# Few-token and heavy expert parts by turns, with a third gate and up buffer and down parts loaded by GpSimd

## The chip, the cores and the metric

The kernel runs on one core of one Trainium2 chip. The metric is the device time of one execution in microseconds, as the median of several runs. The engines are TensorE (PE in the rows), VectorE (DVE), ScalarE (ACT), GpSimd (POOL) and SyncE (SP, which here only issues transfers); PEld is the loading of TensorE's weights.

## What is computed

A two-layer diffusion block on 256 latent and 256 context tokens of width 1024. Each layer has a mixer (attention, pooling, retention) and a channel mixer. The first layer's channel mixer is dense; the second is a mixture of eight experts, of which each token takes two. The change is in the experts alone:

```
def swiglu(t, wg, wu, wd):
    return (jax.nn.silu(t @ wg) * (t @ wu)) @ wd

def moe_ffn(t, router, wg, wu, wd):
    ...
    logits = (tf @ router).astype(jnp.float32)
    top_v, top_i = lax.top_k(logits, TOP_K)
    top_w = jax.nn.softmax(top_v, axis=-1)
    gates = jnp.sum(jax.nn.one_hot(top_i, N_EXPERTS, dtype=jnp.float32) * top_w[..., None], axis=1)
    y = jnp.zeros_like(tf)
    for e in range(N_EXPERTS):
        y = y + gates[:, e:e + 1] * swiglu(tf, wg[e], wu[e], wd[e])
    return y.reshape(shape)
```

All is in float32; `wg` and `wu` are 1024 x 2816, `wd` is 2816 x 1024 for each expert.

## The kernel before

The weights of an expert come in 11 units (`FC`), 88 in all (`NU`). A unit is 256 of the 2816 hidden columns: a gate and up part of 128 x 4096 (2,048 KB, buffers `RGU`, `rgu` in the rows) and a down part of 128 x 2048 (1,024 KB, buffers `RAW`, `raw`). Two buffers of each stand in turn, unit u in buffer u % 2; `load_gu` and `load_d` (lines 1513 to 1521) issue the loads on SyncE's queue, two units ahead, as soon as a buffer is free.

The kernel counts each expert's tokens, sorts the experts by it, and branches (`arms`, line 2528) to a plan that fits the counts. A **heavy** expert has up to 128 tokens in a place. Its weights are split on chip into a high and a low half (`split`: ScalarE copies the high half, VectorE subtracts it for the low half; `ghi`, `glo` for gate and up, three pairs of buffers of 128 x 2048; `dhi`, `dlo` for down, two pairs), and each product is three passes of TensorE (`mm3`): 24 products of 128 x 512 for gate and up and 12 for down in each unit. A **few-token** expert (class `Few`, up to 64 tokens) takes its weights as they are, as the moving operand, with no split.

For each unit there are these steps: `inner` (gate and up products, eight blocks of 128 columns of the input), `act` (silu on ScalarE, times up on VectorE, tile `hx`), `turn` (TensorE flips `hx`; for a heavy unit, `flips`, ScalarE and VectorE then split the flipped tile into `SP`; for a few-token unit VectorE copies it), and `outer` (down products, summed in a PSUM bank over the expert's units). The unit `behind` is the one whose `act`, `turn` and `outer` are still to come; they stand within the next unit's slot.

With the input's counts the plan is: expert 0 alone, in the shadow of other work; `group` (lines 2270 and on), in which expert 1, in two halves, is heavy and experts 2 and 3 are few-token, unit by unit; then `places` (line 2140), which takes experts 4 (few-token), 5 and 6 (heavy) and 7 (few-token) one after the other, 44 units. In `places`, a few-token unit's own `act`, `turn` and `outer` stand in its own slot. A heavy unit's `split_g` and `split_d` stand in its own slot too: the second half of gate and up and the down part are split while TensorE works on the first half, and the down part is used a slot later. Small steps that gather the next expert's tokens or add the last one's result to the residual (generators in `side`, taken by `aside`) are scattered between. Near the end sixteen GpSimd operations (`XT` in the rows) work on the residual.

The order of instructions on each engine is the order in which the program emits them; semaphores and the reuse of buffers make them wait.

Of the kernel before, what the change touches and what calls it, by code (L numbers as in the profile page):

```python
# [36 lines left out]
E = 8  # L37
# [300 lines left out]
def build(tc, a, dbg=None):  # L338
# [1157 lines left out]
    RD = RAW  # L1496
# [21 lines left out]
    def load_d(u):  # L1518
        if u < NU:
            for c in ((slice(0, 1024), slice(1024, 2048)) if u == NU - 1 else (slice(0, 2048),)):  # L1520
                Y.dma_start(RD[u % 2][:, c], src_of(u)[:, 4096:][:, c])
# [11 lines left out]
    def first_d(u):  # L1533
        p = PLACES[u]
        return P5 if u == 5 else AHEAD[p - 2][2] if p > 1 else RD[p]
# [12 lines left out]
    def split_g(u, i, parts=1):  # L1548
        if u < NU:
            q = (2 * part.get(u, u) + i) % 3  # L1550
            n = 2048 // parts
            for j in range(parts):
                c = slice(n * j, n * j + n)
                split(RGU[u % 2][:, 2048 * i:2048 * i + 2048][:, c], GHI[q][:, c], GLO[q][:, c])
                yield ("rest",)
            if i == 1 and not stream:
                load_gu(u + 2)

    def split_d(u, parts=1, eng=None):
        if u < NU:  # L1560
            n = 2048 // parts
            for j in range(parts):
                c = slice(n * j, n * j + n)
                split(RD[u % 2][:, c], DHI[u % 2][:, c], DLO[u % 2][:, c], eng)
                yield ("rest",)
            load_d(u + 2)
# [206 lines left out]
    def gate_up(u, x, ks, b=None):  # L1773
        if b is None:
            b = BK[4 + 2 * (u % 2)]
        for k in ks:
            q = (2 * part.get(u, u) + k // 4) % 3
# [22 lines left out]
    def down_to(acc, w, ht, c):  # L1800
        for kk in range(2):
            for hf in range(2):
                sl = slice(1024 * kk + 512 * hf, 1024 * kk + 512 * hf + 512)
                mm3(acc[hf], ht[:, 0, 128 * kk:128 * kk + 128], ht[:, 1, 128 * kk:128 * kk + 128],
                    DHI[w][:, sl], DLO[w][:, sl], c == 0 and kk == 0, c == FC - 1 and kk == 1)

    def down_e(u, ht):
        s, c = divmod(u, FC)
        down_to(accs(s), u % 2, ht, c)
# [77 lines left out]
    def finish(few, acc, x, rows, last):  # L1887
# [18 lines left out]
        room = RGU[NU % 2]  # L1906
# [234 lines left out]
    def places(todo, side, begun=False):  # L2141
# [10 lines left out]
        def inner(u, ks):  # L2152
            if kinds[u // FC]:
                few_of(u).gate_up((RGU[u % 2][:, :2048], RGU[u % 2][:, 2048:]), ks, bank_of(u))
# [15 lines left out]
        def outer(u):  # L2170
            s, c = divmod(u, FC)
            if kinds[s]:
                few_of(u).down(RD[u % 2], c)
                load_d(u + 2)
            else:
                down_to(accs(s), u % 2, before.pop(), c)
# [10 lines left out]

        behind = None
        for s, few in todo:
            for c in range(FC):  # L2190
# [6 lines left out]
                if not few:  # L2197
                    run(split_g(u, 0, 2))
# [5 lines left out]
                if not few:  # L2204
                    run(split_g(u, 1, 2))
                    rows = split_d(u, 2)
                    next(rows)
                if behind:
                    turn(behind)
                if not few:  # L2210
                    aside(2 if c < 9 else 8)
                inner(u, range(4, 8))
                if not few:
                    run(rows)
                if behind:
                    outer(behind)
                behind = u
                if few:
                    load_gu(u + 2)
                    if u < NU - 1:  # L2220
# [6 lines left out]
                        behind = None  # L2227
                if c == 0 and s > todo[0][0]:
# [21 lines left out]

    def one_hot_few(pos, m):
# [18 lines left out]
    def group(s, few, m, then):  # L2270
# [5 lines left out]
        units = []  # L2276
        for c in range(FC):
            units.append((0, c))
            units += [(1 + i // FC, i % FC) for i in range(len(few) * c, len(few) * c + len(few))]
        stream.update({u0 + i: (([s] + few)[j], c) for i, (j, c) in enumerate(units)})  # L2280
        end = u0 + len(units)
        part.update({u0 + n * c: u0 + c for c in range(FC)})
        nxt = s + 1 + len(few)
        x = nxt % 2
# [19 lines left out]
        def few_in(u, ks):  # L2304
            f.gate_up((RGU[u % 2][:, :2048], RGU[u % 2][:, 2048:]), ks, BK[4])
            if ks[-1] == KT - 1:
                load_gu(u + 2)
                f.swish(BK[4])

        def few_out(u):  # L2310
            f.down(RD[u % 2], units[u - u0][1])
            load_d(u + 2)
# [27 lines left out]
        if s > 1:  # L2340
# [3 lines left out]
            load_gu(u0 + 2)  # L2344
            gate_up(u0, 1, range(4, 8), BK[6])
            run(split_d(u0))
        else:
            one_hot_few(pos_of(few[0]), m)
            from_stash(m)
        swish(BK[6], HX[2])  # L2350
# [24 lines left out]
        for c in range(FC):  # L2375
# [26 lines left out]
            down_to(HEAVY[0][2], u % 2, hts[0], c)  # L2402
# [5 lines left out]
            down_to(HEAVY[1][2], u % 2, hts[1], c)  # L2408
# [10 lines left out]
            if c < FC - 1:  # L2419
                load_gu(u + n + 2)  # L2420
                run(split_d(u + n))
        stream.clear()
        part.clear()
# [112 lines left out]
    def expert_of(s):  # L2536
        eid[s] = nc.values_load(CNTI[0:1, 1, s:s + 1], engines=[ET.SP], min_val=0, max_val=E - 1)

    def parts_of(s):
        for i in range(2):  # L2540
            lookup[FC * s + 1 + i] = nc.values_load(CNTI[0:1, 2 + i, s:s + 1], engines=[ET.SP], min_val=0, max_val=NU - 1)
# [4 lines left out]
    def first_twice():  # L2546
# [10 lines left out]
    load_gu(FC)  # L2557
    load_d(FC)
    parts_of(1)
    load_gu(FC + 1)  # L2560
    load_d(FC + 1)
    arm = arm_of(C1[0:1, 0:1], 7)

    def next_first():
# [3 lines left out]
        for s in (3, 5):  # L2568
            parts_of(s)
# [3 lines left out]
        run(split_d(FC))  # L2573

    few_ends = [(s, s in (4, 7)) for s in (4, 5, 6, 7)]
# [36 lines left out]
```

## Time and profile before

| | |
|---|---|
| median of 3 runs | 1586.68 us (1580.56 to 1586.84) |
| profiled execution | 1585.11 us |
| its span | 1583.3 us |
| TensorE busy | 1460.4 us (92%) |
| VectorE, ScalarE, GpSimd busy | 812.8, 612.7, 93.8 us |
| the group (expert 1 with 2 and 3) | 905 to 1177 us |
| expert 4 (few-token) | 1179.8 to 1269.1 us |
| experts 5 and 6 (heavy) | 1269.1 to 1478.9 us |
| expert 7 (few-token) | 1478.9 to 1563.5 us |
| end of the output | 1583.3 us |

The profiled execution is 1.6 us under the median. Stages are told from the tile names: a product `bk<-rgu,hx` with 64 columns of weights is a few-token unit of experts 4 and 7, `bk<-ghi` a heavy unit. Nearly all rows have the same line, 281, a helper's, so they are read by tile. A few-token product stands as two records in the trace.

### The profile page before, as it was taken

How to read it: one execution, taken by the hardware profiler on the slowest of the kernel's cores; microseconds unless marked ns; L12 is line 12 of the kernel's file. 1: busy time of each engine (PE TensorE's matmuls, PEld its weight loads, DVE VectorE, ACT ScalarE, POOL GpSimd, SP SyncE). 2: the span in 40 equal slices, each digit the busy share in tenths (PEclk: the TensorE clock that was granted, in tenths of full speed). 3: DMA queues.
4: the chain of work that ended last, by engine and by line, in shares of the span. 5: the costliest groups of instructions: out<-in, count | busy, mean ns of one | idle time of the engine just before them, and what ended most of it. 6: DMA issues, size and time to landing. Idle time of an engine off the chain costs nothing. (4 is left out here: it accounts for less than half of the span.)

```text
span 1583.3 us, 25008 instructions
## 1 busy us (share of the span) xinstructions
PE 1460.4 (92%) x10228; PEld 1085.1 (69%) x10228; DVE 812.8 (51%) x1468; ACT 612.7 (39%) x1122; POOL 93.8 (6%) x105
## 2 busy tenths in 40 slices
PE   6989998999999999887988799999998889999986
PEld 4646687887787888674766577777765468877643
DVE  4564446666554353766445542434232087988402
ACT  3465444522223443355542132323320066776201
POOL 2310002000000510100000100000000000000110
PEclk9999999999999999999999899999999999999998
DMA  9535333455765132331479799999989998988894
GB/s 381 181 136 211 107 107 107 133 202 182 255 239 184 56 133 94 115 129 38 161 300 421 283 374 387 352 376 375 359 338 364 389 357 316 364 328 322 326 404 176
DMA packets 45698, 398.35 MB, mean 252 GB/s; under 512 B 5600, under 2 KB 5856, under 8 KB 8960
## 3 DMA queue, kind: packets, MB, share of 16 engines
q1 hardware_dynamic: 44640, 391.98, 65.1%
q0 software_dynamic: 640, 4.26, 0.7%
q8 instruction: 84, 1.38, 0.3%
q10 hardware_dynamic: 288, 0.36, 0.1%
q14 instruction: 46, 0.38, 0.1%
HBM read 395.53 MB, written 1.05 MB: 250 GB/s over the span
## 5 line engine op out<-in xcount | busy, mean ns | idle before, releaser
L281 PE MATMUL b<-HH,wh 128*128 128x512 f32 (+1 forms) x752 | 267.2, 355 | 9.0 <-ACT wh L281 7.5
L281 PE MATMUL b<-HH,wl 128*128 128x512 f32 (+1 forms) x752 | 259.7, 345 | 1.6 <-DVE wl L281 1.5
L281 PE MATMUL b<-HL,wh 128*128 128x512 f32 (+1 forms) x752 | 259.0, 344 | 1.1 <-DVE HL L281 1.1
L281 DVE TENSOR_TENSOR wl<-raw,wh 128x512 fp32r<-128x512 f32 x228 | 151.3, 702 | 130.7 <-ACT wh L281 130.4
L281 ACT ACTIVATE wh<-raw 128x512 fp32r<-128x512 f32 x228 | 131.8, 622 | 183.5 <-DMA raw<-in_fgu_dram 122.0
L281 PE MATMUL bk<-ghi,HL 128*128 128x512 f32 x528 | 181.6, 407 | 8.1 <-ACT ghi L281 8.1
L281 PEld LDWEIGHTS b<-HH,wh 128*128 128x128 f32 x752 | 144.5, 192 | 49.7 <-issue 21.4
L281 DVE TENSOR_TENSOR glo<-rgu,ghi 128x1024 fp32r<-128x1024 f32 x132 | 154.7, 1218 | 16.4 <-ACT ghi L281 16.2
L281 PEld LDWEIGHTS b<-HH,wl 128*128 128x128 f32 x752 | 144.4, 192 | 21.7 <-DVE wl L281 4.6
L281 PEld LDWEIGHTS b<-HL,wh 128*128 128x128 f32 x752 | 144.8, 192 | 17.5 <-DVE HL L281 1.9
L281 DVE TENSOR_TENSOR hx<-hx,bk 128x256 f32<-128x256 f32 (+2 forms) x88 | 29.5, 336 | 235.1 <-ACT hx L281 235.1
L281 ACT ACTIVATE hx<-bk 128x256 f32<-128x256 f32 (+3 forms) x89 | 28.4, 319 | 307.2 <-PE bk L281 307.1
L281 ACT ACTIVATE ghi<-rgu 128x1024 fp32r<-128x1024 f32 x132 | 131.2, 1051 | 18.9 <-DMA rgu<-in_moe_dram 18.8
L281 PEld LDWEIGHTS bk<-ghi,HL 128*128 128x128 f32 x528 | 101.4, 192 | 37.0 <-ACT ghi L281 9.2
L281 PE MATMUL bk<-dhi,SP 128*128 128x512 f32 x352 | 120.1, 402 | 0.0
L281 PE MATMUL b<-h,wh 128*128 128x512 f32 (+1 forms) x384 | 111.9, 375 | 0.0
L281 PE MATMUL bk<-glo,HL 128*128 128x512 f32 x264 | 105.3, 399 | 1.5 <-DVE glo L281 1.3
L281 DVE TENSOR_TENSOR dlo<-raw,dhi 128x1024 fp32r<-128x1024 f32 (+1 forms) x55 | 78.8, 1434 | 15.8 <-ACT dhi L281 15.8
L281 PE MATMUL bk<-rgu,hx 128*32 128x128 f32 (+1 forms) x1376 | 77.2, 305 | 6.5 <-DVE hx L281 3.5
L281 PEld LDWEIGHTS b<-h,wh 128*128 128x128 f32 x384 | 69.8, 188 | 16.4 <-issue 2.5
L281 PEld LDWEIGHTS bk<-rgu,hx 128*32 128x32 f32 (+1 forms) x1376 | 52.9, 118 | 37.8 <-issue 14.1
L281 PEld LDWEIGHTS bk<-dhi,SP 128*128 128x128 f32 x352 | 66.1, 188 | 17.4 <-issue 1.6
(339 smaller groups left out, 2178.3 us busy)
## 6 DMA issues: line engine op xcount, KB each, us to landing
rgu<-in_moe_dram SPq DMA_DIRECT2D x81, 2048.0 KB, 9.5
raw<-in_moe_dram SPq DMA_DIRECT2D x80, 1024.0 KB, 7.2
raw<-in_wmod_dram SPq DMA_DIRECT2D x40, 1024.0 KB, 4.9
raw<-in_fgu_dram SPq DMA_DIRECT2D x22, 1024.0 KB, 5.0
p<-in_moe_dram SPq DMA_DIRECT2D x16, 1024.0 KB, 14.0
raw<-in_wout_dram SPq DMA_DIRECT2D x12, 1024.0 KB, 4.9
raw<-in_fd_dram SPq DMA_DIRECT2D x11, 1024.0 KB, 4.9
raw<-in_wib_dram SPq DMA_DIRECT2D x9, 1024.0 KB, 5.1
```

The costliest lines, as they stand in the source:

```text
L281: r = f(*args, **kw)
```

## The change

The last four experts of this plan (44 units) are taken by turns. `order_by_turns` sets the order of the units: in the first 37 slots, H for heavy and F for few-token, it is `HHFHFHHFHFHHFHFHHFHFHHFHFHHFHFHHFHFHF` (22 H, 15 F; a heavy follows a few-token unit 14 times and a heavy one 7 times), then seven few-token units of expert 7. `by_turns` replaces `places` on this plan. The other parts:

- A third gate and up buffer, two tiles in the room of the second `dhi` and `dlo` pair; it is filled by two loads of 1,024 KB. There is one `dhi`, `dlo` pair now. Buffers are handed on: `done_gu` and `done_d` load the next unit not yet asked for into the buffer that has come free.
- The down parts' loads are issued on GpSimd's queue (`G.dma_start`), so that queue also reads the experts' numbers.
- The down part of a heavy unit is split after that unit's `turn`, in the next slot, instead of in the unit's own slot. `outer` stands between the blocks 4 and 5 and the blocks 6 and 7 of the next unit. Gate and up are split ahead (`take_apart`): half a unit in the few-token slot before, or, before a few-token slot, the unit after it.
- The tokens of experts 4 and 7 are gathered in `tokens_few` directly ahead of their first unit.
- In `group` the down split and the buffers' hand-over follow the new functions, with one `dhi`, `dlo` pair.

```
-    def load_gu(u):
+    at_g, at_d = {}, {}
+    def load_gu(u, i):
+        at_g[u] = i
         if u < NU:
-            for c in ((slice(0, 2048), slice(2048, 4096)) if u == NU - 1 else (slice(0, 4096),)):
-                Y.dma_start(RGU[u % 2][:, c], src_of(u)[:, c])
+            for l, h in ((0, 2048), (2048, 4096)) if i == 2 or u == NU - 1 else ((0, 4096),):
+                Y.dma_start(RGU[i][:, l:h] if i < 2 else GU[i][l // 2048], src_of(u)[:, l:h])
...
+                G.dma_start(RAW[i][:, l:h], src_of(u)[:, 4096 + l:4096 + h])
...
+    def done_gu(u):
+        load_gu(max(at_g) + 1, at_g[u])
...
+    def by_turns(side):
...
+        take_apart(u0, 2)
+        for u in range(u0, NU):
+            s, c = stream[u]
+            last = u == NU - 1
+            if light(u) and c == 0:
+                tokens_few(s)
+            if behind:
+                act(behind)
+            inner(u, range(0, 4))
+            if behind:
+                turn(behind)
+                if not light(behind):
+                    run(split_d(behind, 2))
...
+            aside(4 if u == u0 else 3 if s == 7 and c > 3 else 2)
+            take_apart(u + 1, 2 if light(u) else 1)
+            inner(u, range(4, 6))
+            if behind:
+                outer(behind)
+            inner(u, range(6, 8))
+            if light(u):
+                done_gu(u)
+            take_apart(u + 1, 2)
+            if u + 1 < NU and light(u + 1):
+                take_apart(u + 2, 1)
+            behind = u
+            if s == 7 and c == 5:
+                aside(100)
+                for f in range(KT):
+                    G.tensor_scalar(YT[:, f], YT[:, f], MOD[1][:, 40 + f, 0:1], None, op0=OP.mult)
+                    G.tensor_tensor(XT[:, f, :T], XT[:, f, :T], YT[:, f], OP.add)
...
+    GU = [[t[:, :2048], t[:, 2048:]] for t in RGU] + [[con.tile([128, 2048], F32, name=f"gu{t}", tag=t) for t in ("wh0", "wl0")]]
...
-    DHI, DLO = ([con.tile([128, 2048], F32R, name=f"{n}{i}", tag=f"w{n[1]}{i}") for i in range(2)] for n in ("dhi", "dlo"))
+    DHI, DLO = (con.tile([128, 2048], F32R, name=n, tag=t) for n, t in (("dhi", "wh1"), ("dlo", "wl1")))
```

How the queues change, at three places. ScalarE in the heavy experts, before: one unit's worth, `ghi` a half of gate and up, `hx` the silu of the unit behind, `SP` its flipped tile, `dhi` this unit's down part.

```order
L281 ACTIVATE ghi_8925<-rgu_6257 128x1024 [waits DMAHW5_49,Activation_49]
L281 ACTIVATE ghi_8925<-rgu_6257 128x1024 [waits Activation_49]
L281 ACTIVATE hx<-bk_6474 128x256 [waits PE_49]
L281 ACTIVATE ghi_8926<-rgu_6257 128x1024 [waits Activation_49] x2
L281 ACTIVATE dhi_8930<-raw_78 128x1024 [waits DMAHW6_49,PE_49]
L281 ACTIVATE SP<-bk_6474 128x256 [waits DVE_49,PE_49]
```

After, one heavy slot and the few-token slot behind it (`hx 128x128` is the silu of the few-token unit ahead, at the heavy slot's start; `hx 128x256` is the heavy unit's own, at the few-token slot's start; `ghi` the two halves of the next heavy unit):

```order
L281 ACTIVATE hx<-bk_6474 128x128 [waits PE_49]
L281 ACTIVATE ghi_8928<-rgu_4982 128x1024 [waits DMAHW2_49]
L281 ACTIVATE ghi_8928<-rgu_4982 128x1024
L281 ACTIVATE hx<-bk_6472 128x256 [waits DVE_49,PE_49]
L281 ACTIVATE SP<-bk_6472 128x256 [waits DVE_49,PE_49]
L281 ACTIVATE dhi<-raw_78 128x1024 [waits DMASW1_49,Activation_49]
L281 ACTIVATE dhi<-raw_78 128x1024 [waits Activation_49]
L281 ACTIVATE ghi_8926<-rgu_4982 128x1024 x2
```

The down part's high half has moved from ahead of the flipped tile `SP` of the unit behind to directly after the flipped tile of its own unit, and the first half of the next unit's gate and up, which waits for its transfer, now stands ahead of the silu of the unit before it.

TensorE in the heavy experts, before, from a flip (`CA,hx`) to the down products (`dhi,SP`):

```order
L281 MATMUL bk_6472<-CA,hx 128x128 [waits DVE_49]
L281 MATMUL bk_6472<-CA,hx 128x128
L281 MATMUL bk_6474<-ghi_8926,HL 128x512 [waits Activation_49]
L281 MATMUL bk_6474<-glo_8929,HL 128x512 [waits DVE_49]
L281 MATMUL bk_6474<-ghi_8926,HL 128x512 x2
L281 MATMUL bk_6474<-glo_8929,HL 128x512
L281 MATMUL bk_6474<-ghi_8926,HL 128x512
L281 MATMUL bk_6474<-ghi_8926,HL 128x512 [waits Activation_49]
L281 MATMUL bk_6474<-glo_8929,HL 128x512 [waits DVE_49]
...
L281 MATMUL bk_6470<-dhi_8930,SP 128x512 [waits Activation_49]
L281 MATMUL bk_6470<-dlo_8932,SP 128x512
```

After, in a few-token slot behind a heavy unit (`rgu` with `hx` or `sil` are few-token gate and up products):

```order
L281 MATMUL bk_6472<-rgu_4982,hx 64x256 [waits DMAHW2_49]
L281 MATMUL bk_6472<-rgu_4982,hx 64x256 x7
L281 MATMUL bk_6474<-CA,hx 128x128 [waits DVE_49]
L281 MATMUL bk_6474<-CA,hx 128x128
L281 MATMUL bk_6472<-rgu_4982,sil 64x256 x4
L281 MATMUL bk_6468<-dhi,SP 128x512 [waits Activation_49]
L281 MATMUL bk_6468<-dlo,SP 128x512 [waits DVE_49]
```

Between the flip and the down products twelve heavy products stood before; now four few-token ones do, and the low half `dlo` is waited for.

The transfers, before: gate and up and down parts by turns on SyncE's queue.

```order
L281 DMA raw_78<-in_moe_dram 128x2048 [waits DMAHW2_49,PE_49]
L281 ISA
L281 DMA rgu_4982<-in_moe_dram 128x4096 [waits DMAHW3_49,DVE_49]
L281 ISA
L281 DMA raw_79<-in_moe_dram 128x2048 [waits DMAHW4_49,DVE_49]
```

After, GpSimd's queue near the end, with the down parts of the last units around the residual's sixteen operations:

```order
L281 DMA raw_78<-in_moe_dram 128x2048 [waits DMASW3_49,PE_49]
L281 ISA
L281 DMA raw_79<-in_moe_dram 128x2048 [waits DMASW4_49,PE_49]
L281 TENSOR_SCALAR XT<-XT,MOD_75 128x256 [waits DVE_49,Pool_49]
L281 TENSOR_TENSOR XT<-XT 128x256 [waits Pool_49]
```

The down loads have left SyncE's queue for GpSimd's, where the residual's operations now stand between them.

## Rows read from the trace of the kernel before

**Rows 1.** Stages, core 0: us from:to, length, busy times by engine, clock, DMA share.
```profile
core 0: us, PE busy (x) PEld busy (x) DVE busy (x) ACT busy (x) POOL busy (x), PEclk, DMA share, GB/s
1179.80:1269.10 89.30, 76.54 (x539) 42.45 (x539) 17.72 (x51) 8.58 (x21) 0.00 (x0) 0.98 0.94 365
1269.10:1478.90 209.80, 202.78 (x928) 164.07 (x928) 177.47 (x198) 146.01 (x185) 0.00 (x0) 0.98 0.89 339
1478.90:1563.50 84.60, 74.73 (x538) 41.81 (x538) 10.24 (x30) 7.07 (x18) 13.04 (x16) 0.98 0.89 348
1179.80:1563.50 383.70, 354.05 (x2002) 248.33 (x2003) 205.44 (x279) 161.66 (x223) 13.04 (x16) 0.98 0.90 347
905.00:1177.00 272.00, 271.25 (x2733) 202.87 (x2732) 99.15 (x154) 81.74 (x126) 0.00 (x0) 1.00 0.94 369
```

**Rows 2.** Waits 1179.8 to 1563.5: who waits for whom, us, times, longest.
```profile
PE bk L281 <- DVE hx L281: 16.7, 25, 2.9
...
DVE dlo L281 <- ACT dhi L281: 14.6, 13, 2.5
```

**Rows 3.** The SyncE queue's waits, the same stretch.
```profile
SPq L281 <- PE bk L281: 143.7, 42, 6.6
```

**Rows 4.** SyncE's issues in experts 5 and 6: start, us, what.
```profile
1347.03 0.33 SPq L281 DMA_DIRECT2D raw<-in_moe_dram  x1
...
1355.59 0.33 SPq L281 DMA_DIRECT2D raw<-in_moe_dram  x1
```

**Rows 5.** Timeline of a heavy unit: start, us, operation, idle before it.
```profile
1352.56 0.38 PE L281 MATMUL bk<-CA,hx 128*128 128x128 f32 x2
...
1352.97 0.38 ACT L281 ACTIVATE SP<-bk 128x256 fp32r<-128x256 f32 x1 [2.22 <-PE bk L281]
...
1353.25 1.05 ACT L281 ACTIVATE dhi<-raw 128x1024 fp32r<-128x1024 f32 x1
...
1353.39 0.42 DVE L281 TENSOR_TENSOR SP<-bk,SP 128x256 fp32r<-128x256 f32 x1 [0.38 <-ACT SP L281]
...
1354.33 1.23 DVE L281 TENSOR_TENSOR dlo<-raw,dhi 128x1024 fp32r<-128x1024 f32 x1 [0.52 <-ACT dhi L281]
...
1355.55 0.40 PE L281 MATMUL bk<-dhi,SP 128*128 128x512 f32 x1
```

**Rows 6.** Timeline of TensorE, a few-token unit of expert 7.
```profile
1510.73 0.33 PE L281 MATMUL bk<-CA,hx 128*128 128x128 f32 x1 [0.70 <-DVE hx L281]
1511.44 1.94 PE L281 MATMUL bk<-raw,hx 128*64 128x512 f32 x8 [0.39 <-DVE hx L281]
1513.21 1.90 PE L281 MATMUL bk<-rgu,hx 128*64 128x256 f32 x16
1514.94 1.90 PE L281 MATMUL bk<-rgu,sil 128*64 128x256 f32 x16
1517.53 0.33 PE L281 MATMUL bk<-CA,hx 128*128 128x128 f32 x1 [0.70 <-DVE hx L281]
```

**Rows 7.** Stretches: under GpSimd-issued loads; the best 25 us of the last experts.
```profile
768.00:770.00 2.00, 2.00 (x19) 2.00 (x18) 1.91 (x5) 0.97 (x2) 0.00 (x0) 1.00 1.01 430
...
1250.00:1275.00 25.00, 19.25 (x106) 10.13 (x107) 7.39 (x12) 6.35 (x8) 0.00 (x0) 0.93 1.01 426
```

**Rows 8.** Timeline of TensorE: a gather's products.
```profile
1313.16 1.98 PE L281 MATMUL bk<-og,HH 128*128 128x128 f32 x16
```

**Rows 9.** Loads issued near 876.7 and 1153.1 us: KB, us to landing.
```profile
rgu<-in_moe_dram SPq DMA_DIRECT2D x1, 2048.0 KB, 8.6
...
rgu<-in_moe_dram SPq DMA_DIRECT2D x1, 2048.0 KB, 10.5
```

**Rows 10.** Timeline at the start of expert 5.
```profile
1269.12 4.63 DVE L281 TENSOR_TENSOR glo<-rgu,ghi 128x1024 fp32r<-128x1024 f32 x4 [3.40 <-ACT ghi L281]
...
1269.14 0.51 PE L281 MATMUL bk<-ghi,HL 128*128 128x512 f32 x1 [1.43 <-ACT ghi L281]
```

**Rows 11.** The window of eight products at half clock, 1219.21.
```profile
1219.21:1222.41 3.20, 3.20 (x8) 1.00 (x10) 0.33 (x2) 0.00 (x0) 0.00 (x0) 0.50 0.87 330
```

More of the change, by code (lines that the diff above doesn't have):

```diff
@@ L1549, in split_g @@
         if u < NU:
-            q = (2 * part.get(u, u) + i) % 3
+            q = (2 * heavy(u) + i) % 3
             n = 2048 // parts
@@ L1553, in split_g, with split_d @@
                 c = slice(n * j, n * j + n)
[L1554 removed]
+                split(gu_of(u)[i][:, c], GHI[q][:, c], GLO[q][:, c])
                 yield ("rest",)
[L1556 to L1559 removed]
+            if i == 1 and u > FC:
+                done_gu(u)
+    def split_d(u, parts=1):
         if u < NU:
@@ L1776, in gate_up @@
         for k in ks:
-            q = (2 * part.get(u, u) + k // 4) % 3
+            q = (2 * heavy(u) + k // 4) % 3
             c = slice(512 * (k % 4), 512 * (k % 4) + 512)
@@ L2186, in aside, with take_apart @@
                     side.pop(0)
+        apart = {}
+        def take_apart(u, n):
+            if u < NU and not kinds[u // FC]:
+                while apart.setdefault(u, 0) < n:
+                    run(split_g(u, apart[u], 2))
+                    apart[u] += 1
         behind = None
@@ L2196, in places @@
                     continue
-                if not few:
-                    run(split_g(u, 0, 2))
+                take_apart(u, 2)
                 if behind:
@@ L2249, in places, with order_by_turns @@
         finish(few, accs(E - 1), (E - 1) % 2, rows, last)
+    def order_by_turns():
+        u0 = 4 * FC
+        many_ = [(s, c) for s in (5, 6) for c in range(FC)]
+        few_ = [(s, c) for s in (4, 7) for c in range(FC)]
+        turns = NU - u0 - 7
+        units = []
+        for i in range(turns):
+            units.append((many_ if -(-2 * FC * (i + 1) // turns) > -(-2 * FC * i // turns) else few_).pop(0))
+        units += many_ + few_
+        stream.update({u0 + i: sc for i, sc in enumerate(units)})
+        heavies = [u for u in range(u0, NU) if stream[u][0] in (5, 6)]
+        part.update({u: 2 * FC + i for i, u in enumerate(heavies)})
@@ L2268, in gather_few, with together, group @@
             yield
-    def group(s, few, m, then):
+    def together(s, few):
+        u0, n = FC * s, 1 + len(few)
+        units = []
+        for c in range(FC):
+            units.append((s, c))
+            units += [(few[i // FC], i % FC) for i in range(len(few) * c, len(few) * c + len(few))]
+        stream.update({u0 + i: v for i, v in enumerate(units)})
+        part.update({u0 + n * c: u0 + c for c in range(FC)})
+    def group(s, few, m, then, nxt=None, x=None):
         u0 = FC * s
@@ L2275, in group @@
         n = 1 + len(few)
[L2276 to L2284, printed above, removed]
+        if nxt is None:
+            nxt = s + 1 + len(few)
+            x = nxt % 2
         side = []
@@ L2572, in next_first, with rest, go @@
             gate_up(FC, 1, range(4 * i, 4 * i + 4), BK[6])
-        run(split_d(FC))
-    few_ends = [(s, s in (4, 7)) for s in (4, 5, 6, 7)]
+    buffers = []
+    def rest(*groups, body):
+        def go():
+            if not buffers:
+                buffers.extend((dict(at_g), dict(at_d)))
+            for d, o in zip((at_g, at_d), buffers):
+                d.clear()
+                d.update(o)
+            stream.clear()
+            part.clear()
+            for g in groups:
+                together(*g) if g else order_by_turns()
+            done_gu(FC)
+            body()
+        return go
     def two_groups():
```

186 lines of the change are left out of this document (137 added, 49 removed).

## Prediction

> **What bounds the kernel now.** I read the busy times by stage first. Of the last four experts' 383.70 us TensorE is busy 354.05, so it stands idle 29.65 [rows 1]: 12.76 us in expert 4 (89.30 less 76.54), 9.87 in expert 7 (84.60 less 74.73) and 7.02 in experts 5 and 6 (209.80 less 202.78). The few-token experts move 365 and 348 GB/s with TensorE waiting; the heavy pair moves 339 GB/s with TensorE full. The three-expert group ahead is TensorE's altogether (271.25 of 272.00). The waits say the same: TensorE's largest wait is for VectorE's part of the silu and of the flip (16.7 us), and VectorE's low half of a down part waits for ScalarE's high half, 14.6 us [rows 2], which costs nothing so long as TensorE is elsewhere. The SyncE queue is always early: it stands waiting for a buffer to come free, 143.7 us for TensorE alone [rows 3]. So there is at most some 30 us to be had, by laying transfer-bound parts beside TensorE-bound ones.
>
> Unit prices. A steady heavy unit takes 8.56 us from one down-part issue to the next (1347.03 to 1355.59) [rows 4]; less some 0.2 for the flip, that is 0.232 for each of its 36 products of 128x512. A few-token unit is 1.73 us for the first half of gate and up, the same for the second, 1.77 for down, and 6.81 us from 1510.73 to 1517.53 with its own waits [rows 6].
>
> **Transfers.** 37 slots and a tail of seven few-token units read 44 units of 3.15 MB (2,048 and 1,024 KB), 138 MB in all. Loads issued by GpSimd alone ran at 430 GB/s; the best 25 us here made 426 on SyncE's queue alone [rows 7]. At 426 that is 325 us: transfers would not bind as a whole. Who issues the down parts changes little, since SyncE's issues are 0.33 us each [rows 4]. What changes is that a down load no longer stands behind a gate and up load that waits for its buffer.
>
> **The turn of a heavy unit, the largest new cost.** Before, the down part is split while TensorE computes the second half of the same or next unit: from the flip at 1352.56 the high half's copy starts at 1353.25, the low half follows at 1354.33, and TensorE takes up the down product at 1355.55, about 3.05 us after the flip, with 12 products between, so that the chain is hidden [rows 5]. After, the split of a unit's down part stands on ScalarE and VectorE behind that unit's flip, one slot later, and the down product stands after only two of the four remaining blocks. Between flip and down product TensorE has 0.86 us of work in a few-token slot (1.73 / 2) or 1.38 in a heavy one (6 x 0.23), plus asides. The chain cannot start earlier, as ScalarE takes the flip's copy first. So, on TensorE:
> - few-token slot behind a heavy, 15 times: 1.73 + 3.05 + 2.57 (eleven of the twelve down products) + 0.86 = 8.2, of which 1.8 idle less what asides fill;
> - heavy behind a few-token one, 14 times: 24 x 0.23 + 0.2 + 1.77 = 7.5, no idle;
> - heavy behind heavy, 7 times: 2.78 + 3.05 + 2.57 + 1.38 = 9.8;
> - the first heavy 5.6.
>
> The 37 make 123 + 105 + 69 + 5.6 = 302.6 us.
>
> **Asides and gathers.** About 90 of the asides' 128x128 products fall in slots without a gap, at 1.98 / 16 = 0.124 us each: 11.2. The two gathers of few-token experts are now 32 products each ahead of the first few-token unit, 4.0 us, and the two one-hot writes ahead and copies behind leave TensorE about 1.7 more (two steps the size of the flip's copies, 0.38 and 0.42, on either side) [rows 5, 8]: 11.4 for both. Between 0 and 1.7 for the copies stays open.
>
> **Late gate and up parts.** Where a heavy slot stands between two few-token slots, the next heavy unit's first split goes onto ScalarE and VectorE ahead of the present unit's silu. Its buffer was given back only when the split before the last ended, in the middle of the few-token slot, so its load has about one slot of 7.5 us. A 2,048 KB load landed in 8.6 us at best here and 10.5 under load [rows 9]. VectorE's part of the silu then comes behind one high half (1.05) and two low halves (1.23 each) of the next unit and takes about 0.42 itself [rows 5]: with the gaps between them some 4.05 us after the landing. With 8.6 us I make that 3.5 us for the four whole loads (14) and 1 us for the two halved ones (2): 16. Bounds: nothing, if loads land in 7.5; 4 x 1.9 more at 10.5.
>
> **Start and tail.** The first heavy unit's split waits for the group's last VectorE work, where few-token expert 4 now starts without a split: between 1.43 us (TensorE's wait where expert 5 starts) and 4.63 (its first four low halves) [rows 10]; I take 3. The tail's seven few-token units run at 6.81 to 7.7 (84.60 / 11), say 7.0: 49. The third buffer helps only the first of them. The 16 GpSimd operations on the residual (13.04 us busy [rows 1]) now stand ahead of the down loads of the last four units in GpSimd's queue; each of those is wanted a unit or more later, so I take 0, and 4 us at most. Otherwise a down load on GpSimd waits for the last product out of its buffer, and behind it stands only the next down load. The end (last product to the last store) is unchanged. In the group, one down buffer instead of two costs 0 to 2 us, TensorE having 0.75 us free in 272.
>
> **Clock.** In one few-token unit eight down products fill 3.20 us where 1.77 is usual, at a granted clock of 0.50, the lower level of 1.2 GHz [rows 6, 11]; TensorE had waited for the flip just before. I see four spells like it in the stretch, at 1.6 us lost in each some 7 in all, about what a mean granted clock of 0.98 over 383.70 us says (7.7) [rows 1]. I leave them as they are; the change could remove them or add more where TensorE waits for the chain.
>
> **Sum.** 302.6 + 11.2 + 11.4 + 16 + 3 + 49 = 393.2 us against 383.7: +9.5. The profiled execution took 1585.1 us (1583.3 the span, 1.8 around it), 1.6 under the median of 1586.68, so 1594.6 in its terms and 1596 in the median's. Its own range is 1588 (half of the late loads hidden, 8 us less) to 1605 (those loads at 10.5 us, 7.6 to 9.6 more).
>
> The Trainium skill, page "DMA: Bandwidth & Descriptors", section "Queues, rings and completion order", says that each DMA engine takes turns between the queues it has work for, a packet at a time. By that rule a gate and up load would share the engines with a down load from the other queue where today SyncE's order puts it first, and would land later; no row here shows two queues with large loads at once. That speaks against this change, and is the third rival below.
>
> **Rivals.**
> 1. The asides fill the gaps behind the flips and the loads come in time: 302.6 + 11.4 + 3 + 47.6 (seven at 6.81) = 364.6, or 372 with the clock spells, 12 to 19 us under 383.7: 1568 to 1575, say 1571. For it: TensorE's 354.05 busy us already hold the asides and the spells, and the rings have 25 us stretches at 426 GB/s [rows 7]. Against it: the chain of 3.05 us is in the order of the queues.
> 2. Half of the late loads are hidden, and half of the asides with them: 393 less 8 less 5.6 = 380, 1583.
> 3. Slower. The two queues share the rings, so the four whole loads and the two halved ones land at 10.5 instead of 8.6 and the TensorE waits bring three more half-clock spells: 4 x 1.9 + 2 x 1 + 3 x 1.6 = 14.4 more: 1610. It decides wherever a down load is in flight when a gate and up load with 7.5 us to spare is issued.
> 4. The counts of tokens take an arm that the change leaves alone, and nothing changes: 1587. The stages of before are those of the arm that is changed (one group, then a few-token, two heavy and a few-token expert) [rows 1], so this is unlikely.
>
> **How the numbers follow.** Forecast 0.45, rival 1 0.24, rival 2 0.13, rival 3 0.16, rival 4 0.02. The bound for a measurable difference is 0.5%, 7.9 us: faster below 1578.7, slower above 1594.6. The forecast's own range straddles the upper bound: 0.25 of its chance is slower, 0.20 the same. Rival 1 is faster; of rival 2, 0.01 is faster and the rest the same; rival 3 is slower. Faster 0.25, same 0.34, slower 0.41. The range reaches down to just under rival 1's lower end, 1567, and up to 1608, between the forecast's 1605 and rival 3; the half of rival 3 above it, and what lies under rival 1, stay out.
>
> **What would show it.** In the profile after, few-token slots should have TensorE waiting about 1 us for VectorE's low half of the down part, 15 times, and 7 times in heavy slots; ScalarE's high half of gate and up should wait for its transfer in some six slots, with flips late behind it; the pace per pair of heavy and few-token unit should be near 15.7 us without a late load. I am wrong if TensorE's idle time in the last four experts is below 30 us, if the pair runs at 14.5, or if gate and up loads land above 10 us as a rule.

## The result

The changed kernel takes 1647.08 us (median of 4 runs, 1643.03 to 1651.51) against 1584.78 before: 1.041 times as long, 95% interval 1.039 to 1.043. Forecast were 1596 and a range up to 1608. The sign held; the loss is 62 us where some 10 were forecast, and the time lies outside the range.

The profiled execution took 1651.51 us, the longest of the four (1585.11 before). All of the 66 us lie in the last four experts. First the stretches of the trace after, in the form of [rows 1]: the whole stage, slots 1 to 11, slots 12 to 28, slots 29 and 30 (the second gather and the slot behind it), and the seven few-token units at the end.

```profile
1178.67:1630.45 451.78, 395.24 (x2004) 255.40 (x2004) 209.04 (x282) 157.88 (x216) 35.75 (x59) 0.92 0.75 291
1178.67:1313.95 135.28, 113.74 (x541) 77.86 (x542) 71.01 (x100) 50.75 (x68) 5.28 (x10) 0.89 0.66 248
1313.95:1471.98 158.03, 142.53 (x693) 91.28 (x691) 89.20 (x108) 70.43 (x92) 8.97 (x17) 0.98 0.83 327
1471.98:1504.89 32.91, 27.73 (x121) 19.47 (x119) 11.03 (x16) 7.79 (x11) 1.05 (x2) 0.74 0.56 218
...
1571.08:1630.45 59.37, 51.39 (x372) 29.21 (x368) 7.55 (x22) 4.71 (x12) 16.75 (x23) 0.94 0.74 298
```

The stage grew from 383.70 to 451.78 us, by 68.1. TensorE's idle time grew from 29.65 to 56.54, by 26.9, and its busy time from 354.05 to 395.24, by 41.2, at the same work. The mean granted clock tells most of why it is busy longer: 0.92 instead of 0.98, so by it some 36 us (0.08 x 451.78) were lost to the lower level of 1.2 GHz, against 8 before. Those 28 are not all of the 41.2; the rest is not shown by itself. VectorE and ScalarE have no more to do than before (209.04 and 157.88 against 205.44 and 161.66), and the transfers fell from 347 to 291 GB/s: nothing is full. It is a loss of waits, and of clock with them.

TensorE's own waits in the stage, in the form of [rows 2], and ScalarE's for late weights:

```profile
ACT ghi L281 <- DMA rgu<-in_moe_dram: 36.9, 6, 8.8
...
PE bk L281 <- DVE hx L281: 12.1, 7, 3.2
...
PE bk L281 <- DVE dlo L281: 9.4, 13, 0.8
PE bk L281 <- DVE og L281: 8.9, 4, 4.0
...
PE bk L281 <- DMA raw<-in_moe_dram: 6.6, 2, 6.1
PE bk L281 <- DVE HL L281: 5.3, 2, 4.7
PE bk L281 <- DVE XT L281: 4.9, 4, 3.8
PE bk L281 <- DVE os L281: 4.6, 4, 3.1
```

Before, the one large wait was for `hx`, in 25 short pieces. Now there are seven of some size: `og`, `XT` and `os` are steps of asides, `HL` is a gather's one-hot write. Counting the gate and up products gives each slot's length:

```
                              forecast   usual (measured)   all of them        sum
first heavy                     5.6            -              10.8             10.8
heavy behind heavy, 7           9.8           9.95            9.9 to 16.8      83.2
few-token behind heavy, 15      8.2           8.77            8.7 to 15.9     166.0
heavy behind few-token, 14      7.5           7.87            7.8 to 20.2     132.4
few-token at the end, 7         7.0            -              5.6 to 18.0      59.4
```

The usual slots are near the forecast. What costs the time is the slots that are not usual: the first ten, the three around the second gather, three with late weights, and one of the last seven. The mechanisms, each with its rows:

**The chain behind the flip**, in a usual few-token slot (start, duration, operation, idle before it):

```profile
1436.66 1.95 PE L281 MATMUL bk<-rgu,hx 128*64 128x256 f32 x16
...
1438.54 0.44 PE L281 MATMUL bk<-CA,hx 128*128 128x128 f32 x2
...
1439.02 0.39 ACT L281 ACTIVATE SP<-bk 128x256 fp32r<-128x256 f32 x1 [1.86 <-PE bk L281]
1439.30 1.99 ACT L281 ACTIVATE dhi<-raw 128x1024 fp32r<-128x1024 f32 x2
...
1440.38 2.36 DVE L281 TENSOR_TENSOR dlo<-raw,dhi 128x1024 fp32r<-128x1024 f32 x2 [0.52 <-ACT dhi L281]
1440.40 0.49 PE L281 MATMUL bk<-dhi,SP 128*128 128x512 f32 x1 [0.40 <-ACT dhi L281]
...
1441.66 0.49 PE L281 MATMUL bk<-dlo,SP 128*128 128x512 f32 x1 [0.77 <-DVE dlo L281]
...
1444.41 1.08 PE L281 MATMUL bk<-rgu,sil 128*64 128x256 f32 x8
...
1445.43 0.50 PE L281 MATMUL bk<-ghi,HL 128*128 128x512 f32 x1
```

From the flip to the first product with the low half are 3.12 us (forecast 3.05; the two starts of [rows 5] are 2.99 apart), and TensorE waits twice, 0.40 and 0.77. The slot's four pieces, by their starts, are 1.88, 3.12, 2.75 and 1.02 us, where the forecast had 1.73, 3.05, 2.57 and 0.86.

**An aside behind the split.** In the seventh slot an aside's one-hot write `og` stands on VectorE behind the two low halves of the down part; TensorE reaches the aside's product at 1255.4 and waits for it:

```profile
1256.78 2.36 DVE L281 TENSOR_TENSOR dlo<-raw,dhi 128x1024 fp32r<-128x1024 f32 x2 [0.52 <-ACT dhi L281]
...
1259.06 0.48 DVE L281 TENSOR_SCALAR og<-CA,POSM 128x128 fp32r<-128x128 f32 x2
1259.39 0.69 PE L281 MATMUL bk<-IDR,og 128*128 128x128 f32 x2 [4.01 <-DVE og L281]
```

After it the down products are 0.42 us apart where 0.23 is usual; the stretch from 1259 to 1268 has a granted clock of 0.62:

```profile
1259.00:1268.00 9.00, 8.10 (x24) 6.49 (x25) 3.56 (x8) 0.58 (x1) 0.53 (x1) 0.62 0.82 292
```

**A late gate and up part.** Issued at 1332.27, it lands at about 1341.7; the silu's second half stands behind its split, and the flip behind that:

```profile
1332.27 0.33 SPq L281 DMA_DIRECT2D rgu<-in_moe_dram  x1
...
1341.72 2.00 ACT L281 ACTIVATE ghi<-rgu 128x1024 fp32r<-128x1024 f32 x2 [8.66 <-DMA rgu<-in_moe_dram]
1342.81 2.36 DVE L281 TENSOR_TENSOR glo<-rgu,ghi 128x1024 fp32r<-128x1024 f32 x2 [6.68 <-ACT ghi L281]
...
1345.09 0.41 DVE L281 TENSOR_TENSOR hx<-hx,bk 128x256 f32<-128x256 f32 x1
1345.56 0.69 PE L281 MATMUL bk<-CA,hx 128*128 128x128 f32 x2 [3.03 <-DVE hx L281]
```

**The residual in GpSimd's queue.** Its sixteen operations run from 1584.88 to 1598.59; the down loads behind them go out at 1598.54, and TensorE waits 6.06 us:

```profile
1584.88 0.93 POOL L281 TENSOR_SCALAR XT<-XT,MOD 128x256 f32<-128x256 f32 x1
...
1597.87 0.72 POOL L281 TENSOR_TENSOR XT<-XT 128x256 f32<-128x256 f32 x1
1598.54 1.15 POOL L281 DMA_DIRECT2D raw<-in_moe_dram  x2
...
1609.76 3.68 PE L281 MATMUL bk<-raw,hx 128*64 128x512 f32 x8 [6.06 <-DMA raw<-in_moe_dram]
```

**The clock.** TensorE falls to half clock ten times in this stage. Nine times it is at or behind a wait of 2.66 us or more; behind the waits of 1.60 and 2.07 us it does not fall. The longest stretch, 1484.6 to 1501.5 us, is at the second gather, behind a wait of 4.71: of the 32.91 us of slots 29 and 30 some 8.6 are lost by it (0.26 x 32.91). The tenth has no wait of 1 us ahead of it. It begins among the first gather's products of 128x64, and the few-token products after them take 3.68 us instead of 1.95:

```profile
1201.42 4.26 PE L281 MATMUL bk<-HL,HH 128*128 128x64 f32 x32 [0.55 <-DVE HL L281]
...
1206.16 3.68 PE L281 MATMUL bk<-rgu,hx 128*64 128x256 f32 x16 [0.47 <-ACT hx L281]
```

### The profile page after: what moved, and what is told of

It is laid out like the page before. It is cut to its first block, busy times and chain, and to the rows that moved or that the text cites. A ratio compares the mean times of both kernels' runs of the same rounds, so it can differ in the third digit from the quotient of the medians.

```text
span 1649.9 us, 25097 instructions
## 1 busy us (share of the span) xinstructions
PE 1502.9 (91%) x10228; PEld 1092.9 (66%) x10228; DVE 816.9 (50%) x1470; ACT 609.7 (37%) x1116; POOL 134.8 (8%) x183
## 4 chain that ended last, share of the span: by engine, by line
PE 34%; DVE 6%; issue 4%; DMA 3%; ACT 2%; POOL 1%; DVEq 0%; POOLq 0%; ACTq 0%
PE bk L281 34%; DMA rgu<-in_moe_dram 2%; DVE glo L281 2%; DVE dlo L281 1%; DMA raw<-in_moe_dram 1%; ACT dhi L281 1%; DVE XT L281 1%; POOL XT L281 1%; ACT ghi L281 0%; DVE rgu L281 0%; DVE hx L281 0%; DVE os L281 0%; DVE kept L281 0%; ACT SP L281 0%; DVE SP L281 0%
## 5 line engine op out<-in xcount | busy, mean ns | idle before, releaser
L281 PE MATMUL bk<-ghi,HL 128*128 128x512 f32 x528 | 186.3, 412 | 9.1 <-ACT ghi L281 9.1
L281 DVE TENSOR_TENSOR glo<-rgu,ghi 128x1024 fp32r<-128x1024 f32 x104 | 121.5, 1219 | 37.8 <-ACT ghi L281 37.7
L281 PE MATMUL bk<-dhi,SP 128*128 128x512 f32 x352 | 127.0, 422 | 3.0 <-ACT dhi L281 2.8
L281 ACT ACTIVATE ghi<-rgu 128x1024 fp32r<-128x1024 f32 x104 | 102.6, 1049 | 42.5 <-DMA rgu<-in_moe_dram 36.9
L281 POOL DMA_DIRECT2D raw<-in_moe_dram x78 | 41.3, 529 | 683.9 <-PE bk L281 409.3
L281 PEld LDWEIGHTS bk<-dhi,SP 128*128 128x128 f32 x352 | 70.1, 199 | 30.0 <-ACT dhi L281 10.2
L281 PE MATMUL bk<-dlo,SP 128*128 128x512 f32 x176 | 74.2, 422 | 9.7 <-DVE dlo L281 9.4
## 6 DMA issues: line engine op xcount, KB each, us to landing
rgu<-in_moe_dram SPq DMA_DIRECT2D x56, 2048.0 KB, 10.1
```

The lines of the kernel that those rows point to most:

```text
L281: r = f(*args, **kw)
```

## The experiments

Theory A: the order of the queues makes TensorE wait (the four mechanisms above). Theory B: the two queues of large transfers share the transfer engines, and loads land later. The clock is a third: it could fall for reasons of its own, or only because TensorE waits. Ratios are to the kernel before on the same chip, whose medians lie between 1580.90 and 1584.78 us; the differences to 1647 are between medians of runs on several chips, so some 4 us of each are open.

**Down part split early**

```
 by_turns:
                 turn(behind)
-                if not light(behind):
-                    run(split_d(behind, 2))
...
             if behind:
                 outer(behind)
+            if not light(u):
+                run(split_d(u, 2))
             inner(u, range(6, 8))
```

> The changed kernel, with one step moved: a heavy unit's down part is split in the unit's own slot, right behind the down products of the unit behind, instead of behind its own flip a slot later. Theory A (the chain flip, high half, low half, down product, and what stands behind it in the queues, makes the loss): few-token slots behind a heavy one go from 8.77 to about 7.3 us and heavy behind heavy from 9.95 to about 9, some 30 us of 1647 go, to about 1617. Theory B (the loss is in the transfers, which land later since two queues share the engines): nothing here changes a load, 1640 to 1650.

1625.02 us (1.0275 times before, 1.0234 to 1.0317): 22 less. Usual slots came to 7.28 and 8.77 us, as theory A has it; but in seven slots the flip now waited 1.8 to 4.3 us, with the silu behind the down split on ScalarE. In two of them (4.28 and 3.95) the down part, wanted earlier, has not landed yet. In four (1.81 each) it has landed, by 0.4 us or more, and the split waits for TensorE's last products out of the one `dhi`, `dlo` pair that the third gate and up buffer has left. In the seventh (3.21) it waits for neither. Some of the gain was given back there. ScalarE's waits before the down split in this run:

```profile
ACT dhi L281 <- PE bk L281: 24.4, 11, 6.6
...
ACT dhi L281 <- DMA raw<-in_moe_dram: 7.3, 4, 4.9
```

**The last four down parts issued by SyncE**

```
-                G.dma_start(RAW[i][:, l:h], src_of(u)[:, 4096 + l:4096 + h])
+                (Y if u >= NU - 4 else G).dma_start(RAW[i][:, l:h], src_of(u)[:, 4096 + l:4096 + h])
```

> The changed kernel, with the down parts of the last four units issued on SyncE's queue, so that they do not stand behind the sixteen residual operations in GpSimd's queue. If those operations hold the loads up, TensorE's wait of 6.06 us in the last units goes, with the half-clock spell behind it: 9 to 13 us less, about 1636. If the wait is for bandwidth or for the free buffer, it stays: 1645 to 1650.

1638.38 us (1.0347, 1.0319 to 1.0374): 9 less, as expected of the hold-up: TensorE's wait for a down part is gone, and the slot that held it went from 18.0 to 9.5 us.

**Asides ahead of the flip**

```
             inner(u, range(0, 4))
+            aside(4 if u == u0 else 3 if s == 7 and c > 3 else 2)
             if behind:
                 turn(behind)
...
-            aside(4 if u == u0 else 3 if s == 7 and c > 3 else 2)
```

> The changed kernel, with the asides emitted ahead of the flip and the down split instead of behind them. Theory A (an aside's VectorE step stands behind the low half of the down part, and TensorE waits 4.0 us for it, in four or five slots): 15 to 25 us less, with the half-clock spells that follow these waits, about 1627. Rival: the asides only push the flip and its chain back by what they gain: 1642 to 1652.

1634.15 us (1.0321, 1.0293 to 1.0349): 13 less. The waits for `og` are gone; the seventh and eighth slots went from 16.8 and 14.0 us to 11.1 and 9.9. The gain is a little under what was expected.

**No half unit split ahead of a few-token slot**

```
-            if u + 1 < NU and light(u + 1):
-                take_apart(u + 2, 1)
```

> The changed kernel, without the split of half a unit ahead of a few-token slot, so that the silu of the heavy unit behind no longer stands behind a split that waits for its transfer. Theory A: the waits of 3.0, 2.1 and 3.2 us before a flip and the 4.7 ahead of the second gather go, but the next heavy unit's split has to be done within the few-token slot: 5 to 15 us less, about 1637. Theory B (loads late whatever waits for them): the wait moves to the start of the heavy slot, 1645 to 1655.

1634.43 us (1.0313, 1.0280 to 1.0347): 13 less. The slots with the late weights went from 13.2, 10.9 and 13.8 to 8.8 us, the second gather's from 20.2 to 12.9, and no heavy slot waits for its split but the first. TensorE's waits for `hx` fell from 12.1 us to:

```profile
PE bk L281 <- DVE hx L281: 3.4, 7, 0.9
```

So these loads come in time for the products; they were late for a split that stood ahead of other work.

**All four**

> The changed kernel with all four edits together: down part split in the unit's own slot, asides ahead of the flip, no half unit split ahead of a few-token slot, the last four down parts issued by SyncE. One at a time they took 22, 9, 13 and 13 us off 1647. Theory A (independent faults of the queues' order): 57 us less, about 1590, within 10 of the kernel before. Rival (they share the same waits, or transfers bind as soon as TensorE runs faster): 1605 or more, with TensorE waiting for rgu or raw.

1603.77 us (1.0139, 1.0109 to 1.0170): 43 less, where the four add up to 57. What was left is the wait that the early split brought: a down part that lands while ScalarE stands at its split, with the silu and the flip behind.

```profile
1345.67 2.00 ACT L281 ACTIVATE dhi<-raw 128x1024 fp32r<-128x1024 f32 x2 [6.18 <-DMA raw<-in_moe_dram]
...
1349.50 0.44 PE L281 MATMUL bk<-CA,hx 128*128 128x128 f32 x2 [2.98 <-DVE hx L281]
```

**Two more edits on top of the four**

```
+                if not light(behind) and behind not in early:
+                    run(split_d(behind, 2))
+            if u + 1 < NU and light(u + 1) and stream[u + 1][1] == 0:
+                hot_few(stream[u + 1][0])
...
-            if not light(u):
+            if not light(u) and (behind is None or light(behind)):
                 run(split_d(u, 2))
+                early.add(u)
```

> The kernel with all four edits, and two more for the waits that were left there (a flip that waits 2 to 3 us behind a down part that has not landed, where two heavy units follow each other, and a gather that waits 2.7 us for its one-hot write): the down part of a heavy unit behind a heavy one is split in the next slot, behind the silu, and the one-hot write is emitted a slot earlier. Theory A: 10 to 18 us less than 1604, about 1590. Rival (the wait moves to the down product): 1600 to 1606.

1584.78 us, 1.0024 times before (1.0000 to 1.0049): 19 less again, and level with before. At this pace the transfers seem to bind in one place: among the last units TensorE waits 3.63 us for a down part that was issued at 1520.29 and lands 13.2 us later, while the transfers run at 424 GB/s (433 from 1510 to 1520); no run shows this by itself.

```profile
1510.00:1515.00 5.00, 5.00 (x35) 3.25 (x34) 1.65 (x3) 1.65 (x3) 0.00 (x0) 1.00 1.03 433
1515.00:1520.00 5.00, 4.60 (x32) 2.60 (x32) 2.17 (x4) 0.00 (x0) 0.00 (x0) 1.00 1.02 433
...
1530.00:1535.00 5.00, 1.37 (x4) 0.59 (x6) 0.00 (x0) 0.00 (x0) 4.75 (x7) 0.68 1.00 424
...
1533.63 3.68 PE L281 MATMUL bk<-raw,hx 128*64 128x512 f32 x8 [3.63 <-DMA raw<-in_moe_dram]
```

**GpSimd issues the down loads in the kernel before** (one part alone: `Y.dma_start` becomes `G.dma_start` in `load_d`, and GpSimd also reads the experts' numbers)

> The kernel before, with nothing changed but the engine that issues the down parts' loads in the last seven experts: GpSimd instead of SyncE. Theory B (two queues share the transfer engines, and loads land late): 10 us or more above before. Theory A: 0 to 5 us, from the residual's operations in GpSimd's queue alone.

1585.61 us (1.0026, 1.0005 to 1.0047): 0.26% more, 0.47% at most. Its gate and up loads land in 9.9 us (9.5 before):

```profile
rgu<-in_moe_dram SPq DMA_DIRECT2D x81, 2048.0 KB, 9.9
raw<-in_moe_dram POOLq DMA_DIRECT2D x76, 1024.0 KB, 7.7
```

**SyncE issues all loads in the changed kernel** (`G.dma_start` becomes `Y.dma_start`)

> The changed kernel, with all down parts issued on SyncE's queue as before. Theory B: gate and up loads land sooner than the changed kernel's 10.1 us, and 10 to 30 us go. Theory A: the gain is that of the last four units alone, some 9 us, less what the down loads lose behind gate and up loads that wait for a buffer: 1636 to 1655.

1641.25 us (1.0368, 1.0338 to 1.0397): 6 less, where the last units' hold-up gave 9 by itself. The gate and up loads land sooner, in 9.3 us instead of 10.1, but no gain shows beyond theory A's; the 10 to 30 us of theory B do not come, nor its 10 us with two queues in the kernel before.

```profile
rgu<-in_moe_dram SPq DMA_DIRECT2D x56, 2048.0 KB, 9.3
raw<-in_moe_dram SPq DMA_DIRECT2D x80, 1024.0 KB, 8.4
```

**The late down split in the kernel before**

```
 places:
-                    rows = split_d(u, 2)
-                    next(rows)
                 if behind:
                     turn(behind)
+                    if not kinds[behind // FC] and behind != FC:
+                        run(split_d(behind, 2))
...
-                inner(u, range(4, 8))
-                if not few:
-                    run(rows)
+                inner(u, range(4, 6))
                 if behind:
                     outer(behind)
+                inner(u, range(6, 8))
...
```

> The kernel before, with its sequence of experts and its buffers, but with the down part of a heavy unit split behind that unit's flip and its down products between the blocks 4 and 5 and the blocks 6 and 7 of the next unit. It gives the chain's price by itself: by the steady slots of the changed kernel (9.95 us for heavy behind heavy) against 8.56 before, 21 times 1.4 us: about 29 us above before, 1612. If the chain were hidden by what runs ahead on ScalarE, less than 10.

1613.82 us (1.0193, 1.0160 to 1.0227): 32 more than before, 29 expected. The steady heavy unit takes 9.83 us, near the 9.95 expected, from one down load's issue to the next, against 8.56 in [rows 4]:

```profile
1365.81 0.33 SPq L281 DMA_DIRECT2D raw<-in_moe_dram  x1
...
1375.64 0.33 SPq L281 DMA_DIRECT2D raw<-in_moe_dram  x1
```

But this is not the chain's price alone, and the agreement is luck. Counting the gate and up products here too, nine units go from some 8.57 to 9.85 us, 11 us together; nine others grow by less than 1 us or not at all. The remaining four take 14.7 to 17.1 us where they took 10.3 to 14.1, 16 more together: there a step that stands behind the late split (`os` and `SP` in the waits) makes TensorE wait 2.9 to 4.0 us, and the clock falls (0.96 in the heavy experts, 0.98 before). So the asides behind the split cost more than the chain, in this order of units.

```profile
PE bk L281 <- DVE os L281: 7.9, 2, 4.0
PE bk L281 <- DVE dlo L281: 7.9, 12, 0.8
PE bk L281 <- ACT SP L281: 5.9, 2, 2.9
```

**The turns taken back, with and without the four edits**

```
-        for i in range(turns):
-            units.append((many_ if -(-2 * FC * (i + 1) // turns) > -(-2 * FC * i // turns) else few_).pop(0))
-        units += many_ + few_
+        units = few_[:FC] + many_ + few_[FC:]
```

> The changed kernel with the order of its units set back to that of before: expert 4, then 5 and 6, then 7, everything else as changed (steps within a slot, third buffer, GpSimd's loads). Theory A': what the turns themselves do (loads that come late in bursts, asides that meet splits) is the larger part: 21 heavy units behind a heavy one at 9.95 us, the few-token experts at some 8 us a unit, and the residual's hold-up at the end: about 1610 to 1620. If the order of steps within a slot is the whole loss, the turns being harmless: 1640 or more.

1615.06 us (1.0212, 1.0163 to 1.0262): 32 less than the changed kernel. So the turns make about half of the loss with this order of steps; what else is changed makes the other half, and the late down split by itself gave nearly as much (32 us) in the kernel before.

> The kernel with all four edits, its units in the order of before. Against the run with all four edits by turns (1604) it shows what the turns are worth once the queues are in order. If they are worth what the steady slots say (a heavy and a few-token unit 15.1 us by turns, 16.5 one after the other, 15 pairs): 1615 or more. If asides, gathers and late parts eat that: 1590 to 1605.

1593.76 us (1.0072, 1.0046 to 1.0099), 10 less than the same code by turns (1603.77). The gain that the steady slots promise (15.1 us a pair against 16.5, 15 pairs) does not arrive even there. The 16.5 hold in this run, but as 9.70 and 6.77: its heavy units take 9.70 us, not the 8.56 of before, and TensorE waits 0.95 for the silu in each. So this is not the best that the old order of units can do, and the two further edits were not run in it.

**A wait priced by itself**

```
                 if not few:
                     run(split_g(u, 0, 2))
+                    if c in (2, 5, 8):
+                        for _ in range(6):
+                            S.activation(GHI[2 * part.get(u, u) % 3][:, :1024], RGU[u % 2][:, :1024], AF.Copy)
```

> The kernel before, with ScalarE made to copy the first quarter of a heavy unit's high half six times over (6 x 1.05 us, the same values into the same place) in six of the 22 heavy units, which makes TensorE wait some 3 to 6 us each time. It prices a wait by itself, in the order of before. If TensorE's clock has no part, the time grows by the sum of the added waits, some 18 to 36 us, and the count of half-clock spells (four in this stretch) stays. If a wait of that length brings the clock down, spells follow the waits, and the time grows by 1.7 us more for each spell of 3.4 us.

1620.50 us against 1580.90 on the same chip (1.0242, 1.0194 to 1.0290): 39.6 more. TensorE's six new waits are 2.55, 4.93, 4.77, 4.01, 4.96 and 4.78 us, 26.0 together (the row's seventh, 1.4, is there before too), so 13.6 us came on top; by the ratio's interval it is 5 to 20, and in the two profiled executions, 36.1 apart, 10.1. TensorE's other waits in the stage are those of before. Behind each of the six, the one of 2.55 too, it runs at half clock for 3 to 7 us (here the second), and the stage's mean granted clock is 0.92, where it is 0.98 in [rows 1]:

```profile
PE bk L281 <- ACT ghi L281: 27.4, 7, 5.0
...
1323.00:1328.00 5.00, 0.42 (x2) 0.00 (x0) 0.00 (x0) 4.87 (x5) 0.00 (x0) 0.85 0.35 147
1328.00:1333.00 5.00, 4.66 (x11) 3.69 (x12) 3.88 (x4) 3.40 (x5) 0.00 (x0) 0.50 0.15 29
...
1269.10:1515.00 245.90, 213.65 (x914) 170.81 (x914) 175.68 (x195) 181.78 (x219) 0.00 (x0) 0.92 0.75 281
```

So a wait of 2.5 to 5 us cost some 0.4 to 0.5 of its length again in clock. These six falls of the clock come from waits that were put in; the one behind the first gather of the changed kernel shows that a long wait is not its only cause.

## Why the prediction was wrong, step by step

The sum was 393.2 us for the stage; it took 451.8. The 58.6 us between them, term by term:

- **The chain, right in kind, a little small.** 302.6 us for the 37 slots becomes 317.0 at the measured usual lengths (14 x 7.87 + 15 x 8.77 + 7 x 9.95 + 5.6): 14.4 too little. The flip-to-product time was right (3.05 against 3.12), and so was the steady heavy unit with it in the order of before (9.83 us). In the slot shown above the other three pieces are 0.15 to 0.18 us longer each than forecast; that this comes from the changes between the two kinds of products, which the sum took as joining without a gap, is likely but not shown by itself.
- **Asides, mis-sized, the step that failed first.** I priced them as 90 products of 0.124 us. An aside is a chain: one-hot write on VectorE, product, copy on VectorE, product. After, its VectorE step stands behind the down split, which stands behind the flip. The first ten slots are 43 us over their usual lengths, where my terms (asides, the first gather, the start) gave some 20; the asides' waits of 3.8, 4.0, 4.0 and 3.1 us, 14.9 together, and the clock (0.11 x 135.28, again 14.9) more than cover the difference. The products were counted right and the queue they stand in was not looked at, though rival 1 even had them fill gaps.
- **Late gate and up parts, right in kind and near in size.** 16 us were forecast for 6 places; flips waited 1.6, 3.0, 2.1 and 3.2 us, behind a split that waited for its load, and the second gather 4.7. Taking the early split away gave 13. The 8.6 us were not the best landing: in the last four experts before they run from 7.3 to 12.4 us.
- **The clock, put at nothing: the largest single miss.** The text leaves the four spells as they are, some 7 us, but the sum has no term for them: its slots are all at full clock. The clock took some 36 us (they are within the sizes of the other points). I had the row with a half-clock spell after a wait, and I listed more waits, and did not put a price on them. With the 0.4 to 0.5 measured on top of each us waited, in waits of 2.5 to 5 us, my 16 us of late parts alone would have been 22 to 24.
- **GpSimd's queue, wrong.** I took 0, and 4 at most, for the residual's operations, on the ground that the loads behind them are wanted a unit or more later. The shortest of the last units take 5.6 us, not 7.0: their flip and down products stand a slot later, and the waits of 0.70 and 0.39 in [rows 6] are gone from TensorE's rows between 1584.70 and 1590.28. So the 13.7 us of operations are over two units long. The wait was 6.06 us, with a half-clock spell, and its removal gave 9. The tail's seven units took 59.4 us, 49 forecast.
- **Start, right.** TensorE's first waits for the split are 2.66, just ahead of the stage as measured, and 0.76; 3 were forecast.

Of the rivals: the first (1571) needed the asides to fill the gaps; they lengthened them. The third (slower, 1610) had the side right and more half-clock spells behind waits, but by way of shared transfer engines, and the runs with one queue and with two give that no such price. The Trainium skill, page "DMA: Bandwidth & Descriptors", section "Queues, rings and completion order", has the engines take turns between queues; the runs agree with it so far as gate and up loads land 0.4 to 0.8 us later with a second queue, and show that in the kernel before this is worth 0.26% of the time, 0.47 at most. The trace before did show two queues at once, which the prediction missed: in the first stretch of [rows 7], read as GpSimd's loads alone, a load of 1,024 KB on SyncE's queue, issued at 765.86, is in flight, which lands after 10.3 us where 4.9 is the median of its kind. Of the three signs I named for being wrong one was met: gate and up loads land at 10.1 us in the median. It pointed at the transfers, which were not the cause. The other two looked for a faster kernel only: TensorE's idle time is 56.54 us, not below 30, and the pair of a heavy and a few-token slot takes 16.6 us, 15.7 forecast, not 14.5.

Slot by slot the measured stage is 317.0 us of usual slots, 43 over in the first ten, 17 in the three around the second gather, 12 in three with late parts, 3 in two with asides, and 59 at the end: 451, clock included.

What stays open: how the waits and the clock share the loss of the changed kernel cannot be separated further here, since no run had its long waits without the clock. The third gate and up buffer and the one `dhi`, `dlo` pair that pays for it were not tried alone. The edits' gains overlap (57 us one at a time, 43 together). No version ran faster than the kernel before; the nearest is level with it.

## What to carry to other kernels

When a step is moved behind another engine's result, everything that stands behind it in the in-order queues moves too: price an aside by the queue it waits in, not by its products. In this kernel a wait of TensorE of 2.5 to 5 us cost about 1.4 to 1.5 times its length, because the clock fell behind it; a sum made of steady slots at full clock needs a term for that. When the total of an experiment comes out as expected, look whether it comes from the places that were expected: here 32 us for 29 came in about half from elsewhere. And a gain that the steady slots promise (1.4 us a pair) has to pay for the slots that are not steady; count those first.

## What the runs showed of the hardware that was not expected

Six waits of 2.55 to 4.96 us, put into a stretch where TensorE is otherwise full, brought 10.1 us (profiled executions) to 13.6 us (medians) over their own 26.0, with half clock behind each. The Trainium skill, page "TensorE: Matmul & The Clock Gate", section "HAM oscillation — how this bites in real kernels", tells of the same with waits for transfers; here the waits were for ScalarE, and the trace agrees.

Moving 81 MB of loads from SyncE's queue to GpSimd's changed the time by 0.26% (0.05 to 0.47), with the loads of the other queue landing in 9.9 us instead of 9.5.
